# Stacked queries and doubled keys in a differential attention, with two background lanes paced anew

## The chip, the cores and the metric

The kernel runs on one core of one Trainium2 chip. The metric is the device time of one execution in microseconds (us). The core has five engines: TensorE for matrix products, VectorE, ScalarE, GpSimd and SyncE, the last of which only issues transfers here. In the profile they are PE (products) and PEld (weight loads), DVE, ACT, POOL and SP.

## What is computed

Two blocks in sequence on 512 tokens of width 1024, in float32. The first block has two layers: windowed attention, a short convolution and a state-space model (SSM) as three gated branches, then a gated feed-forward network. The second block, which the change mostly touches, has one layer: a gated linear unit into a causal depthwise convolution of 31 taps with a layer norm, beside it a causal differential attention, both gated and merged, then a feed-forward network.

```python
u = ua * jax.nn.sigmoid(ub)
u = conv31(u) + conv_b;  u = silu(layer_norm(u));  y_conv = u @ conv_w_out + conv_b_out
q1, q2, k1, k2 = rope(...)                      # 8 heads of 64 each
a = softmax(q1 k1^T) - lam * softmax(q2 k2^T)   # causal, per head
att = rms_norm(a @ v)                           # v: 8 heads of 128
y = (g_conv * y_conv + g_att * att) @ w_o
```

## The kernel before, in words

**Split products.** A float32 matrix is split into a rounded part h and a rest l, and a product is made of three: hh, hl and lh (`mm3`, line 467, products at lines 470 to 472). A split is one ScalarE rounding (line 380) and one VectorE subtraction (line 383). Weights come as units of 128x1024 through three buffers (`_fetch`, line 421); for most units of the second block's first half (`BESIDE`) the rest is made by two ScalarE operations and an accumulating transfer issued on GpSimd's queue, without VectorE.

**Buffers.** 78 slots of 128x512 float32 are handed out by `big` from a list of free ones, first freed first used. Eight PSUM banks are handed out by `psum`.

**The second block** (`second`, line 1372). The unit `w_in_2` gives the convolution's inputs (16 units). Then come four parts (line 1458), two heads of v each. In a part, 32 split products of 512 columns give the part's 4 query halves and 4 key halves (a block of 128 tokens by 8 x 64), `rope2` (line 1662) rotates them in place, 32 split products of 256 columns give v, and the part's attention is queued. After the fourth part stand 16 gates of 8 split products, then the eight output products of the convolution (conv_out), which read the normed convolution `cn`, then `w_o_2`.

**Lanes.** Convolution and attention run beside these products as Python generators, a step at a time. Every group of three products is a beat, every third beat a tick (`beat`, line 474; `tick`, line 496). At each tick a lane gains its rate as credit and does a step for each whole credit. `finish` runs all that is left of a lane at once. The lane conv (one generator at a time) holds eight `convolve` (line 1379; a step is three VectorE operations, ten steps each) and `conv_norm` (line 1771; 17 steps). The lane att (two at a time, by turns) holds for each part a `_diff_turn` (line 1680) and four `_diff_block` (line 1693). The rates are the constants of line 17: conv runs at R3 = 0.6 and R4 = 0.6, at R5 = 0.8 from the gates on; att at R2 = 1.0 and R6 = 1.5 from conv_out on. `finish("conv")` stands before conv_out (line 1499), `finish("att")` before conv_out's seventh output.

**Attention.** `_diff_turn` transposes the rotated 128x512 tiles, 16 transposes of 128x128 a part (line 1684), and splits the four results (two with queries, two with keys; a result holds two heads, one on the lower and one on the upper 64 rows). `_diff_block` n handles query block n against the n + 1 key blocks, w = 128 (n + 1) columns. For each of two s it makes three products a head on 64 rows (line 1712), alternating between two heads:

```python
for i, (x, y) in enumerate(((0, 0), (0, 1), (1, 0))):
    for e in range(2):
        rows = slice(64 * e, 64 * e + 64)
        nc.tensor.matmul(ps[e][:, :w], qk[s][x][rows, tn], qk[2 + s][y][rows, :w], start=i == 0, stop=i == 2)
```

Masks (line 552), exponentials, transposes of the probabilities (line 1736), products with v (line 1744), a norm and a last transpose (line 1762) follow.

**In the first block** the windowed attention stacks h and l of a query on 128 rows and multiplies them with keys that stand twice on 128 rows, two products a head (lines 993 and 994). The SSM (`ssm`, line 1152) spreads its input over partitions by 16 copies of 32x128, eight on ScalarE and eight on VectorE (line 1176), for each of four quarters ct.

**Order.** The program text is not the order of the engines' instructions. The kernel is built with a scheduler that orders every engine but SP's queue ahead of time, by text order among what its own timeline holds for ready. At run time each engine's order is fixed.

Of the kernel before, what the change touches and what calls it, by code (L numbers as in the profile page):

```python
# [16 lines left out]
R1, R2, R3, R4, R5, R6 = 0.9, 1.0, 0.6, 0.6, 0.8, 1.5  # L17
# [3 lines left out]
NTB = 4  # L21
# [290 lines left out]
class Net:  # L312
# [839 lines left out]
    def ssm(self, L, ct, u, tabs, ys2):  # L1152
# [18 lines left out]
        for i in range(4):  # L1171
            for j in range(4):
                o = uu[32 * j:32 * j + 32, i]
                s = u[32 * i:32 * i + 32, j::4]
                if j % 2:
                    nc.vector.tensor_copy(out=o, in_=s)  # L1176
                else:
                    self.act(o, s)
            if i == 1:
                yield  # L1180
# [191 lines left out]
    def second(self, follow, out):  # L1372
# [6 lines left out]
        def convolve(i):  # L1379
            acc = self.big(f"acc{i}")  # L1380
            self.act(acc, us[i], AF.Identity, scale=self.cw[:, 31 * i + 30:31 * i + 31], bias=self.p("conv_b", i))
            for j in range(29, -1, -1):
                s = 30 - j
                self.stt(acc[:, s:], us[i][:, :512 - s], self.cw[:, 31 * i + j:31 * i + j + 1], acc[:, s:], ALU.mult, ALU.add)
                if j % 3 == 0:
                    yield
            self.free(us[i])
            conv.append(acc)
            if i == 1:
                csum.append(self.big("csum"))  # L1390
                self.add(csum[0], conv[0], conv[1])
            elif i > 1:
                self.add(csum[0], csum[0], acc)

        csum, cn = [], []
        cl = self.lane("conv", 1, R3)
# [60 lines left out]
        self.lane("conv", 1, R4)  # L1457
        for part in range(4):
            pq = [self.psum(f"pq{t}") for t in range(NTB)]
# [11 lines left out]
            self.free(pq)  # L1471
            for t in range(NTB):
                self.rope2(ra[t], cos[:, t], sin[:, t])
# [18 lines left out]
            al.waiting += self.diff_attention(part, ra, vv, ya, done)  # L1492
            if part == 3:
                cl.waiting.append(self.conv_norm(conv, csum, cn))
                self.lane("conv", 1, R5)
# [4 lines left out]
        self.lane("att", 2, R6)  # L1500
# [161 lines left out]
    def rope2(self, a, cos, sin):  # L1662
# [9 lines left out]
        self.add(a, a, b)  # L1672
        self.free(b)

    def diff_attention(self, part, ra, vv, ya, done):
        qk = []
        left = [NTB]
        return [self._diff_turn(ra, qk)] + [self._diff_block(part, n, qk, vv, ya, left, done) for n in range(NTB)]

    def _diff_turn(self, ra, qk):  # L1680
        for j in range(4):
            pt = self.psum("qkT", (128, 4, 128))
            for t in range(NTB):
                self.nc.tensor.transpose(pt[:, t], ra[t].rearrange("p h d -> p (h d)")[:, 128 * j:128 * j + 128], self.ident)
            h, l = self.big("qkh", F32R), self.big("qkl", F32R)
            self.split(h, l, pt.rearrange("p t d -> p (t d)"))
            self.free(pt)
            qk.append((h, l))
            if j == 3:
                self.free(ra)  # L1690
            yield

    def _diff_block(self, part, n, qk, vv, ya, left, done):
        nc = self.nc
        while len(qk) < 4:
            yield
# [7 lines left out]

        pp = [[self.big("dp"), self.big("dp")] for _ in range(2)]
        mx = [self.small("dmx", (128, 2), bufs=4) for _ in range(2)]
        for s in range(2):
            ps = [self.psum("dsc") for _ in range(2)]
            for i, (x, y) in enumerate(((0, 0), (0, 1), (1, 0))):
                for e in range(2):  # L1710
                    rows = slice(64 * e, 64 * e + 64)
                    nc.tensor.matmul(ps[e][:, :w], qk[s][x][rows, tn], qk[2 + s][y][rows, :w], start=i == 0, stop=i == 2)  # L1712
# [17 lines left out]
        if n == NTB - 1:  # L1730
            self.free(qk)
# [39 lines left out]
    def conv_norm(self, conv, csum, out):  # L1771
        while len(conv) < 8:
            yield
        s = csum[0]
# [76 lines left out]
```

## Time and profile before

| | us |
|---|---|
| median of 3 runs | 2483.45 |
| lowest, highest | 2479.06, 2487.06 |
| profiled execution, its own time | 2489.97 |
| its span, first to last instruction | 2488.2 |
| PE busy in the span | 2442.6 |
| DVE busy | 1594.7 |
| ACT busy | 1111.5 |
| POOL busy | 362.5 |

Products overlap in the pipe: a product that the trace shows for 0.39 us starts 0.23 us after the one before. What a product takes is thus read from start to start. Mean granted clock of TensorE is 0.992 of full speed.

### The profile page before, as it was taken

How to read it: one execution, taken by the hardware profiler on the slowest of the kernel's cores; microseconds unless marked ns; L12 is line 12 of the kernel's file. 1: busy time of each engine (PE TensorE's matmuls, PEld its weight loads, DVE VectorE, ACT ScalarE, POOL GpSimd, SP SyncE). 2: the span in 40 equal slices, each digit the busy share in tenths (PEclk: the TensorE clock that was granted, in tenths of full speed). 3: DMA queues.
4: the chain of work that ended last, by engine and by line, in shares of the span. 5: the costliest groups of instructions: out<-in, count | busy, mean ns of one | idle time of the engine just before them, and what ended most of it. 6: DMA issues, size and time to landing. Idle time of an engine off the chain costs nothing.

```text
span 2488.2 us, 32578 instructions
## 1 busy us (share of the span) xinstructions
PE 2442.6 (98%) x12206; PEld 2054.3 (83%) x12206; DVE 1594.7 (64%) x3010; ACT 1111.5 (45%) x2034; POOL 362.5 (15%) x870
## 2 busy tenths in 40 slices
PE   8999999999999999999999999999999999999998
PEld 6888888888888888888888788988887769988887
DVE  7898855544455489875677744688788466643435
ACT  5467433322233365743432222544656765634222
POOL 7824000000037063200000000001111110000000
PEclk9999999999999999999999999999999989999999
DMA  4222233223233322123366632367646543122232
GB/s 154 80 77 69 77 123 106 93 94 102 93 99 109 120 70 79 60 102 121 130 208 223 216 120 94 116 168 182 147 102 140 119 106 119 69 93 89 93 106 77
DMA packets 90879, 282.80 MB, mean 114 GB/s; under 512 B 10336, under 2 KB 11744, under 8 KB 90720
## 3 DMA queue, kind: packets, MB, share of 16 engines
q1 hardware_dynamic: 83520, 254.50, 30.5%
q0 software_dynamic: 7200, 26.22, 6.2%
q8 instruction: 95, 1.56, 0.2%
q14 instruction: 64, 0.52, 0.1%
HBM read 274.39 MB, written 6.29 MB: 113 GB/s over the span
## 4 chain that ended last, share of the span: by engine, by line
PE 80%; DVE 7%; DMA 6%; issue 3%; ACT 2%; POOL 2%; SPq 1%; DVEq 0%; POOLq 0%; ACTq 0%
PE bank L470 25%; PE bank L471 25%; PE bank L472 25%; DMA slot<-in_wada_dram 4%; DVE slot L383 2%; DVE wl L383 2%; ACT slot L380 2%; PE bank L1712 1%; DVE slot L401 1%; DMA raw<-in_w_dram 1%; POOL s_w L383 1%; POOL slot L383 1%; PE bank L1744 1%; DVE slot L1176 0%; PE bank L1202 0%
## 5 line engine op out<-in xcount | busy, mean ns | idle before, releaser
L470 PE MATMUL bank<-slot,wh 128*128 128x512 f32 x2456 | 964.3, 394 | 7.8 <-ACT slot L380 7.6
L472 PE MATMUL bank<-slot,wl 128*128 128x512 f32 x2456 | 959.8, 391 | 4.2 <-DMA wl<-in_w_dram 2.1
L471 PE MATMUL bank<-slot,wh 128*128 128x512 f32 x2456 | 960.2, 391 | 0.0
L380 ACT ACTIVATE wh<-raw 128x1024 fp32r<-128x1024 f32 (+3 forms) x369 | 385.2, 1045 | 767.4 <-PE bank L471 390.6
L470 PEld LDWEIGHTS bank<-slot,wh 128*128 128x128 f32 x2456 | 463.4, 189 | 105.1 <-ACT slot L380 8.3
L472 PEld LDWEIGHTS bank<-slot,wl 128*128 128x128 f32 x2456 | 462.6, 188 | 104.5 <-DVE wl L383 4.9
L471 PEld LDWEIGHTS bank<-slot,wh 128*128 128x128 f32 x2456 | 463.4, 189 | 95.9 <-issue 1.7
L383 DVE TENSOR_TENSOR wl<-raw,wh 128x1024 fp32r<-128x1024 f32 (+3 forms) x319 | 390.9, 1226 | 203.0 <-ACT wh L380 201.6
L383 DVE TENSOR_TENSOR slot<-bank,slot 128x512 f32<-128x512 f32 (+4 forms) x340 | 197.6, 591 | 239.9 <-PE bank L472 208.7
L380 ACT ACTIVATE slot<-slot 128x512 fp32r<-128x512 f32 (+3 forms) x378 | 207.9, 558 | 288.9 <-DVE slot L383 265.9
L383 DVE TENSOR_TENSOR slot<-slot,slot 128x512 f32<-128x512 f32 (+4 forms) x480 | 287.0, 617 | 51.0 <-ACT slot L380 47.5
L380 ACT ACTIVATE slot<-bank 32x128 f32<-32x128 f32 (+8 forms) x398 | 183.2, 473 | 96.9 <-PE bank L472 34.5
L471 PE MATMUL bank<-wl,slot 128*128 128x512 f32 (+1 forms) x480 | 182.4, 380 | 4.3 <-DVE wl L383 4.3
L472 PE MATMUL bank<-wh,slot 128*128 128x512 f32 (+1 forms) x480 | 181.5, 379 | 0.0
L470 PE MATMUL bank<-wh,slot 128*128 128x512 f32 (+1 forms) x480 | 181.4, 380 | 0.0
L470 PE MATMUL bank<-slot,slot 128*128 128x256 f32 (+1 forms) x624 | 177.9, 293 | 2.1 <-ACT slot L380 2.1
L471 PE MATMUL bank<-slot,slot 128*128 128x256 f32 (+1 forms) x624 | 179.0, 291 | 0.5 <-DVE slot L401 0.5
L472 PE MATMUL bank<-slot,slot 128*128 128x256 f32 (+1 forms) x624 | 178.3, 289 | 0.0
L401 DVE SCALAR_TENSOR_TENSOR slot<-slot,slot 128x512 f32<-128x512 f32 (+1 forms) x184 | 123.9, 688 | 84.7 <-DMA slot<-in_wada_dram 57.2
L401 DVE SCALAR_TENSOR_TENSOR slot<-slot,cw,slot 128x485 f32<-128x485 f32 (+24 forms) x240 | 166.6, 732 | 4.2 <-ACT slot L380 2.4
L383 DVE TENSOR_TENSOR slot<-slot,bank 128x512 f32<-128x512 f32 (+1 forms) x104 | 66.1, 643 | 131.0 <-PE bank L472 131.0
L470 PEld LDWEIGHTS bank<-slot,slot 128*128 128x128 f32 x624 | 118.2, 193 | 4.4 <-ACT slot L380 2.7
(199 smaller groups left out, 2263.7 us busy)
## 6 DMA issues: line engine op xcount, KB each, us to landing
raw<-in_w_dram SPq DMA_DIRECT2D x373, 512.0 KB, 3.3
wl<-in_w_dram POOLq DMA_DIRECT2D x50, 512.0 KB, 5.6
slot<-in_wada_dram SPq DMA_DIRECT2D x96, 256.0 KB, 4.9
raw<-in_w_dram SPq DMA_DIRECT2D x32, 448.0 KB, 3.3
slot<-in_x_dram SPq DMA_DIRECT2D x16, 256.0 KB, 3.9
xd<-slot SPq DMA_DIRECT2D x16, 256.0 KB, 6.2
slot<-xd SPq DMA_DIRECT2D x16, 256.0 KB, 3.5
out_dram<-slot SPq DMA_DIRECT2D x8, 256.0 KB, 2.0
```

The costliest lines, as they stand in the source:

```text
L380: return self.nc.scalar.activation(out=out, in_=in_, func=func, scale=scale, **kw)
L383: return (eng or self.nc.vector).tensor_tensor(out=out, in0=a, in1=b, op=op)
L401: return self.nc.vector.scalar_tensor_tensor(out=out, in0=a, scalar=s, in1=b, op0=op0, op1=op1, **kw)
L470: t.matmul(ps, ah, bh, start=start, stop=False)
L471: t.matmul(ps, ah, bl, start=False, stop=False)
L472: t.matmul(ps, al, bh, start=False, stop=stop)
L1712: nc.tensor.matmul(ps[e][:, :w], qk[s][x][rows, tn], qk[2 + s][y][rows, :w], start=i == 0, stop=i == 2)
L1744: nc.tensor.matmul(po[:, e], at[e][:, b], vv[b // 2][:, b % 2, 128 * e:128 * e + 128], start=b == 0, stop=b == n)
```

## The change

Scores: the transposed queries are stored with h on one half of the rows and l on the other (`qs`), the keys are doubled on both halves before they are transposed (`kd`), and a head's score is two products on 128 rows. `_diff_turn` now makes 24 transposes a part and eight splits of 512 columns, four of them on 64 rows, in six steps (four before). `rope2` writes queries to half of a slot (two token blocks share one) and doubled keys to a slot each, and the projection's buffer is freed at once.

Pacing: att runs at R2 = 1.5 throughout. Conv runs in each part at the steps left over the ticks left up to 14 ticks into the gates, from the gates on at the steps left over 14, and at 0.7 once `conv_norm` begins.

First block: for ct = 0 all 16 copies of the SSM's input are on ScalarE.

```diff
-R1, R2, R3, R4, R5, R6 = 0.9, 1.0, 0.6, 0.6, 0.8, 1.5
+R1, R2, R3 = 0.9, 1.5, 0.6
...
-                if j % 2:
+                if j % 2 and ct:
                     nc.vector.tensor_copy(out=o, in_=s)
...
                 if j % 3 == 0:
+                    steps[0] -= 1
                     yield
...
+        steps = [80]
...
-        self.lane("conv", 1, R4)
         for part in range(4):
+
+            cl.rate = steps[0] / (16 * (4 - part) + 14)
...
+            qd, kd = [], []
             for t in range(NTB):
-                self.rope2(ra[t], cos[:, t], sin[:, t])
+                if t % 2 == 0:
+                    qd.append(self.big("qd", shape=(128, 2, 4, 64)))
+                kd.append(self.big("kd", shape=(128, 4, 2, 64)))
+                self.rope2(ra[t], qd[t // 2][:, t % 2], kd[t], cos[:, t], sin[:, t])
+                self.free(ra[t])
...
-                self.lane("conv", 1, R5)
+                cl.rate = steps[0] / 14
...
         self.finish("conv")
-        self.lane("att", 2, R6)
...
-        self.add(a, a, b)
+        self.add(q, a[:, 0:4], b[:, 0:4])
+        k, kb = (z[:, 4:8].unsqueeze(2).to_broadcast([128, 4, 2, 64]) for z in (a, b))
+        self.add(kd, k, kb)
...
+        for s in range(2):
+            pt = self.psum("qT", (128, 4, 128))
             for t in range(NTB):
-                self.nc.tensor.transpose(pt[:, t], ra[t].rearrange("p h d -> p (h d)")[:, 128 * j:128 * j + 128], self.ident)
...
+                self.nc.tensor.transpose(pt[:, t], qd[t // 2][:, t % 2, 2 * s:2 * s + 2].rearrange("p h d -> p (h d)"), self.ident)
+            src = pt.rearrange("p t d -> p (t d)")
+            qs = [self.big("qs", F32R) for _ in range(2)]
+            for e in range(2):
+                rows, rest = slice(64 * e, 64 * e + 64), slice(64 - 64 * e, 128 - 64 * e)
+                self.act(qs[e][rows], src[rows])
+                self.sub(qs[e][rest], src[rows], qs[e][rows].bitcast(F32))
             self.free(pt)
+            ks = []
+            for e in range(2):
+                yield
+                pt = self.psum("kT", (128, 4, 128))
+                for t in range(NTB):
+                    self.nc.tensor.transpose(pt[:, t], kd[t][:, 2 * s + e].rearrange("p i d -> p (i d)"), self.ident)
+                ks.append((self.big("kh", F32R), self.big("kl", F32R)))
+                self.split(*ks[e], pt.rearrange("p t d -> p (t d)"))
+                self.free(pt)
+            qk.append((qs, ks))
...
-            for i, (x, y) in enumerate(((0, 0), (0, 1), (1, 0))):
-                for e in range(2):
-                    rows = slice(64 * e, 64 * e + 64)
-                    nc.tensor.matmul(ps[e][:, :w], qk[s][x][rows, tn], qk[2 + s][y][rows, :w], start=i == 0, stop=i == 2)
+            for e in range(2):
+                for i in range(2):
+                    nc.tensor.matmul(ps[e][:, :w], qk[s][0][e][:, tn], qk[s][1][e][i][:, :w], start=i == 0, stop=i == 1)
...
     def conv_norm(self, conv, csum, out):
         while len(conv) < 8:
             yield
+        self.lanes["conv"].rate = 0.7
```

## Rows read from the trace of the kernel before

**Rows 1.** The page: busy us, share of the span, instructions.

```profile
PE 2442.6 (98%) x12206; PEld 2054.3 (83%) x12206; DVE 1594.7 (64%) x3010; ACT 1111.5 (45%) x2034; POOL 362.5 (15%) x870
```

**Rows 2.** Table by stretch: length, busy us (instructions), TensorE's granted clock, DMA.

```profile
1712.00:1976.00 264.00, 263.98 (x1456) 216.24 (x1455) 195.22 (x441) 155.30 (x333) 35.74 (x40) 1.00 0.56 129
1976.00:2000.00 24.00, 14.94 (x82) 11.61 (x81) 15.66 (x37) 20.31 (x45) 3.61 (x4) 0.79 0.32 74
2000.00:2066.00 66.00, 61.16 (x271) 45.64 (x270) 39.41 (x96) 39.65 (x92) 6.07 (x7) 0.96 0.48 132
```

**Rows 3.** TensorE's timeline, 1978 to 2066: start, length, instruction, [idle before, who ended it].

```profile
1992.08 0.69 PE L1712 MATMUL bank<-slot,slot 64*128 64x128 f32 x4 [4.50 <-DVE slot L383]
...
1995.62 0.80 PE L470 MATMUL bank<-slot,wh 128*128 128x512 f32 x1 [1.88 <-ACT slot L380]
...
2064.07 1.18 PE L1744 MATMUL bank<-slot,slot 128*128 128x128 f32 x6 [2.61 <-ACT slot L380]
```

**Rows 4.** TensorE's timeline, 1792 to 1797: six score products, then three.

```profile
1792.79 0.40 PE L472 MATMUL bank<-wh,slot 128*128 128x512 f32 x1
1793.12 0.96 PE L1712 MATMUL bank<-slot,slot 64*128 64x512 f32 x6
1794.01 0.50 PE L470 MATMUL bank<-wh,slot 128*128 128x512 f32 x1
...
1795.51 0.39 PE L470 MATMUL bank<-wh,slot 128*128 128x512 f32 x1
1795.83 0.96 PE L1712 MATMUL bank<-slot,slot 64*128 64x512 f32 x3
1796.72 0.50 PE L471 MATMUL bank<-wl,slot 128*128 128x512 f32 x1
```

**Rows 5.** Table by stretch, the products of line 1712 alone.

```profile
1712.00:2066.00 354.00, 37.32 (x192) 22.12 (x192) 0.98 0.53 125
```

**Rows 6.** TensorE's timeline, 129 to 132: stacked products of the first block's attention.

```profile
129.91 0.28 PE L993 MATMUL bank<-slot,slot 128*128 128x256 f32 x1
...
130.87 0.40 PE L470 MATMUL bank<-slot,wh 128*128 128x512 f32 x1
131.10 0.40 PE L471 MATMUL bank<-slot,wh 128*128 128x512 f32 x1
```

**Rows 7.** TensorE's timeline, 1746: four transposes of the turning and what follows.

```profile
1746.44 0.60 PE L1684 MATMUL bank<-cst,slot 128*128 128x128 f32 x4
1746.80 0.48 PE L470 MATMUL bank<-wh,slot 128*128 128x512 f32 x1
```

**Rows 8.** Groups by form, VectorE and ScalarE: busy us, mean ns | idle before.

```profile
L383 DVE TENSOR_TENSOR slot<-bank,slot 64x512 fp32r<-64x512 f32 x16 | 11.0, 688 | 1.2 <-ACT slot L380 0.8
L383 DVE TENSOR_TENSOR slot<-slot,slot 128x256 f32<-128x256 f32 x32 | 12.0, 417 | 1.1 <-ACT slot L380 1.1
L380 ACT ACTIVATE slot<-bank 64x512 fp32r<-64x512 f32 x16 | 9.5, 591 | 2.8 <-DVE slot L383 2.2 <-PE bank L963 0.4
```

**Rows 9.** Table by stretch, before and after the convolution's end.

```profile
1650.00:1920.00 270.00, 270.00 (x1461) 223.45 (x1459) 229.35 (x453) 146.64 (x281) 36.74 (x41) 1.00 0.62 146
1920.00:1980.00 60.00, 59.98 (x300) 47.51 (x300) 25.88 (x80) 41.12 (x94) 8.46 (x10) 1.00 0.62 134
```

**Rows 10.** VectorE's timeline: the copies for ct = 0 in layers 0 and 1.

```profile
42.37 8.29 DVE L1176 COPY slot<-slot 32x128 f32<-32x128 f32 x8
...
829.13 2.22 DVE L1176 COPY slot<-slot 32x128 f32<-32x128 f32 x8
```

**Rows 11.** Table by stretch around the copies of layer 0.

```profile
36.00:52.00 16.00, 12.44 (x56) 10.07 (x54) 11.99 (x13) 10.45 (x19) 16.00 (x56) 0.96 0.03 10
```

**Rows 12.** TensorE's timeline there.

```profile
52.70 0.79 PE L471 MATMUL bank<-wl,slot 128*128 128x512 f32 x1 [4.26 <-DVE wl L383]
```

**Rows 13.** ScalarE's timeline there.

```profile
39.87 4.23 ACT L380 ACTIVATE slot<-slot 128x512 f32<-128x512 f32 x9
```

**Rows 14.** All instructions that read the convolution's taps `cw`: min/median/max ns, first and last start.

```profile
L401 DVE SCALAR_TENSOR_TENSOR slot<-slot,cw,slot x240: 689/732/752, 1634.2 to 1919.2; 128x503 f32<-128x503 f32 x7, 128x497 f32<-128x497 f32 x7, 128x495 f32<-128x495 f32 x7, 128x493 f32<-128x493 f32 x7
```

More of the change, by code (lines that the diff above doesn't have):

```diff
@@ L1491, in second @@
                 ya[m] = self.big(f"ya{m}")
-            al.waiting += self.diff_attention(part, ra, vv, ya, done)
+            al.waiting += self.diff_attention(part, qd, kd, vv, ya, done)
             if part == 3:
                 cl.waiting.append(self.conv_norm(conv, csum, cn))
-                self.lane("conv", 1, R5)
+                cl.rate = steps[0] / 14
             for m in range(sum(GATES[:part]), sum(GATES[:part + 1])):
@@ L1671, in rope2, with diff_attention, _diff_turn @@
         self.mul(a, a, tab(cos))
-        self.add(a, a, b)
+        self.add(q, a[:, 0:4], b[:, 0:4])
+        k, kb = (z[:, 4:8].unsqueeze(2).to_broadcast([128, 4, 2, 64]) for z in (a, b))
+        self.add(kd, k, kb)
         self.free(b)
-    def diff_attention(self, part, ra, vv, ya, done):
+    def diff_attention(self, part, qd, kd, vv, ya, done):
         qk = []
         left = [NTB]
[L1678 to L1682, printed above, removed]
+        return [self._diff_turn(qd, kd, qk)] + [self._diff_block(part, n, qk, vv, ya, left, done) for n in range(NTB)]
+    def _diff_turn(self, qd, kd, qk):
+        for s in range(2):
+            pt = self.psum("qT", (128, 4, 128))
             for t in range(NTB):
-                self.nc.tensor.transpose(pt[:, t], ra[t].rearrange("p h d -> p (h d)")[:, 128 * j:128 * j + 128], self.ident)
-            h, l = self.big("qkh", F32R), self.big("qkl", F32R)
-            self.split(h, l, pt.rearrange("p t d -> p (t d)"))
-            self.free(pt)
-            qk.append((h, l))
-            if j == 3:
-                self.free(ra)
+                self.nc.tensor.transpose(pt[:, t], qd[t // 2][:, t % 2, 2 * s:2 * s + 2].rearrange("p h d -> p (h d)"), self.ident)
[5 more added lines that the diff above has]
+                self.sub(qs[e][rest], src[rows], qs[e][rows].bitcast(F32))
+            self.free(pt)
+            ks = []
[8 more added lines that the diff above has]
+            qk.append((qs, ks))
+            if s == 1:
+                self.free(qd, kd)
             yield
@@ L1694, in _diff_block @@
         nc = self.nc
-        while len(qk) < 4:
+        while len(qk) < 2:
             yield
@@ L1730, in _diff_block @@
         if n == NTB - 1:
-            self.free(qk)
+            self.free([[q, k] for q, k in qk])
         at = []
```

2 lines of the change are left out of this document (1 added, 1 removed).

## The prediction

> **What bounds the kernel now.** I read the page's busy shares first: TensorE is busy for 98% of the span [rows 1], so a microsecond counts only if it comes off TensorE's own row of products or off one of its few waits. The change sits almost wholly in one stage, so next comes the table by stretch from the first query-key product of the second block (1712) to the last product of conv_out (2066) [rows 2]. Up to 1976 TensorE is never idle (263.98 of 264). From 1976 to 2000 it works 14.94 of 24 us at a mean granted clock of 0.79, from 2000 to 2066 61.16 of 66 at 0.96. That is 9.1 + 4.8 = 13.9 us idle. The clock costs at most 24 x 0.21 + 66 x 0.04 = 7.7 us more, part of it inside the idle time; I count 4. So about 18 us are lost at the end of the stage. The TensorE timeline names the waits [rows 3]: 4.50 us for VectorE in the middle of a score product, 1.88 us for ScalarE before conv_out's first product at 1995.62, 2.61 us for ScalarE among the last attention blocks. The reader is to see two regimes: a long stretch in which only TensorE's work counts, and a short end in which waits count too.
>
> **Where the end comes from.** The step counts of the lanes follow from the code. A convolution is 8 x 10 steps and its norm 17; an attention part has 4 steps of turning and 6 for each of 4 blocks, and a few idle steps. A tick is three beats: 16 ticks a part, 43 in the 16 gates. At rates 0.6 and 0.8 the gates begin with 54 convolution steps issued and end with 80, plus 9 of the norm; attention (1.0) stands at 48 and then 91 of 121. So finish("conv") empties 8 norm steps in one go, and conv_out, whose input they are, waits; 28 attention steps lie under conv_out and the last ones are emptied at once before m = 6. That is the timeline's picture: the norm chain and part 3's first blocks contend at 1980 to 1996, the last blocks at 2061.
>
> **Part 1, the score products.** Today each pair of heads takes six products on 64 rows. Six at 512 columns started together hold the array from 1792.79 (start of the product before) to 1794.01 (start of the one after), less one normal interval of 0.23: 0.99 us. Three alone, one head's share, hold it from 1795.51 to 1796.72: 0.98 us [rows 4]. So pairing is free when it happens, and often it doesn't: the engines' order is set ahead of time and splits many pairs. The whole x192 hold 37.32 us [rows 5]. After the change there are 128 products over all 128 rows, of the form that the first block's attention uses already (lines 993 and 994): eight of 256 columns run from 129.91 to 130.87, 0.12 each, and a 512-column product takes 0.23 (130.87 to 131.10) [rows 6]. With 0.12 for 128 columns too (a bound from above) and 0.17 for 384 (halfway), four products cost 0.48, 0.48, 0.68 and 0.92 for n = 0 to 3, 2.56 together, times 8 (two s, four parts) = 20.5 us. Gain 37.3 - 20.5 = **16.8 us**, all on the path. Bounds: were every pair undivided today, the groups would cost 0.99 / 0.92 x 20.5 = 22 us by the 512-column one, so the gain is at least 1.5 us; at the top, 0.11 instead of 0.12 for the narrow ones gives 17.5.
>
> One rule of the Trainium skill speaks against this part. TensorE: Matmul & The Clock Gate, Part 3 (Packing small matmuls), says that products on different row groups run at the same time, starting some 4 ns apart. By it six half-height products cost three intervals, 3 x (0.12 + 0.12 + 0.17 + 0.23) x 8 = 15.4 us, and the change would lose 5 us instead of gaining 17. The trace agrees with the concurrency but not with the price: 0.99 us against 3 x 0.23 [rows 4], because the first product starts 0.33 after its predecessor, not 0.23 (1792.79 to 1793.12), and three alone are no cheaper than six. By the skill's other page on it, TensorEngine Tiling (Array Packing), Key Properties, a change of tiling mode drains the engine; that would be such a delay.
>
> **Part 2, the transposes.** Doubled keys make 24 transposes a part of 16: 32 more. Four of them take 0.36 us (1746.44 to 1746.80) [rows 7], 0.09 each, and with 0.12 as the upper end **+3.4 us** at 0.105.
>
> **Part 3, more VectorE and ScalarE work.** Turning grows from four splits to eight a part, so 16 more subtractions at 688 ns (11 us) and 16 more activations at 591 ns (9.5 us); writing the queries apart adds 16 additions of 128x256 at 417 ns (6.7 us) [rows 8]; the doubled-key addition replaces the old 512-column one. TensorE covers this as long as VectorE keeps pace. VectorE works 229.35 of 270 us (85%) from 1650 to 1920 while TensorE is idle for nothing, and then only 25.88 of 60 [rows 9]: the convolution is through, and attention is issued too slowly to use it. Slots are used more heavily too (twelve of split operands for eight, six of rotated ones for four, though a rotated buffer is freed at once). No row shows a slot wait by itself; bounds are 0 and one 4.50-us wait [rows 3] a part, 18 us. I take 0, since TensorE had no idle time while two parts were in flight.
>
> **Part 4, the pacing.** With attention at 1.5 and the convolution at what is left over what remains (0.82 in part 0, 0.83 later, 0.79 in the gates), the gates begin with 69 convolution steps and 74 attention steps and end with 80, all 17 of the norm (three ticks before) and all 137 of attention. So nothing is emptied in one go at finish("conv"), and conv_out runs without attention beside it: the 2.61-us wait goes, and most of the 1980 to 1996 burst. What is late next is the tail of the norm: its last step is issued three ticks (some 8 us) ahead of conv_out and is a chain of six operations of the size of those in [rows 8]. Of the 18 us I take **12** away (bounds 0 and 18). The new price is VectorE's. Its need from 1650 to conv_out's first product is now 229.4 + 25.9 + some 10 = 265 us; 18 come with the new work, and 18 with the attention moved ahead of conv_out (about half of the 39.41 us in 2000 to 2066 [rows 2]): 301 us. The stretch is 1995.6 - 1650 = 346 us today, plus 17 for the attention moved in (66 less 4.8 idle less 192 products at 0.23), less 16.8, plus 3.4, less the 9.1 of waits: about 341. VectorE must hold 88% where it held 85% unhurried. For that I add **+2 us** (bounds 0 and +15).
>
> **Part 5, the copies of the first block.** For ct = 0 eight VectorE copies a layer go to ScalarE. In layer 0 the eight take 8.29 us, in layer 1 2.22 us [rows 10]; GpSimd works without a gap during the first, 16.00 of 16 us [rows 11]. The split of a weight stands behind them on VectorE, and TensorE waits 4.26 us for it [rows 12]. ScalarE's nine operations, eight of them copies, took 4.23 us there [rows 13], so eight more take 3.8, and the weight's rounding behind them slips by up to that: the wait moves to ScalarE but shrinks. I take **-4 us**, bounds -7 (the whole wait, with the clock at half for what follows) and +1.
>
> **The sum.** -16.8 + 3.4 - 12 + 2 - 4 = -27.4 us. On the profiled execution (2489.97 us, of which the span is 2488.2) that gives 2462.6; it lies 6.5 above the median of the runs shown, so on the median 2483.45 - 27.4 = **2456 us**.
>
> **Rivals.** (a) The end stays as it is. The engines' order is set ahead from readiness, not from the lanes alone: the last of the convolution's products began at 1919.2 [rows 14], some 30 us before the lanes had issued the last of them. If pacing moves little, or VectorE holds only its 85% (301 / 0.85 = 354 us, 13 later), the gain is 16.8 - 3.4 + 4, less 0 to 4: 2466 to 2470. For it: 88% is above anything in the table. Against: both lanes end earlier by count. Chance 0.24. (b) The change doesn't do what it says: half-height pairs would have run at three intervals (the rule above), scores and transposes cost 8.5 us, pacing gives 12 and copies 4, less 2: 2478, no measurable change. Against it stand the 37.32 us. Chance 0.03; with other ways to within 0.3%, 0.07. (c) Slower: VectorE becomes the bound. The convolution, issued a third faster, fills VectorE's queue; masks, splits and the norm line up behind it, and TensorE's queue, which runs in order, stands at scores or at conv_out. From 1712 to 2066 VectorE's mean share is 250.3 / 354 = 71% [rows 2]; at that share 301 us need 424, 83 more than the stretch has, and the result is 2456 + 81 = 2537. It decides below 301 / (341 + 35) = 80%, where 2491 is reached. For it: order on an engine is fixed, and one late result holds all behind it. Against: from 1650 to 1920 the same mix held 85% with no wait. Chance 0.06. Upside (d): the whole end and the whole copy wait vanish: 2445, chance 0.13 for 2441 to 2448.
>
> **How the numbers follow.** Forecast 0.50 (2448 to 2464), (d) 0.13, (a) 0.24, same 0.07, slower 0.06. The range 2441 to 2472 holds the forecast, (d) and most of (a). A measurement of this kernel tells about 0.3% (7.5 us) from no change, so faster means below 2476: 0.87, same 0.07, slower 0.06.
>
> **What would show it.** In the profile after: no products of 64 rows, x128 full-height ones with about 20 us; 96 transposes at the turning line; VectorE's low share from 1920 to 1980 gone; TensorE busy and at full clock up to conv_out, no attention after it; at 48 to 53 us a shorter wait, now for ScalarE. I am wrong if VectorE shows over 90% before conv_out and TensorE waits for it, or if the waits at conv_out's first product are as long as before.

## The result and the profile after

The changed kernel takes 2503.76 us (median of 4 runs, 2501.22 to 2504.58) against 2483.74 us for the kernel before: a ratio of 1.0078 [1.0061, 1.0094]. It is about 20 us **slower**; forecast were 2456 us and a gain of 27. The profiled execution has a span of 2502.0 us, 13.8 more than before.

The page of the changed kernel, busy time by engine (before in [rows 1]):

```profile
PE 2437.4 (97%) x12174; PEld 2061.6 (82%) x12174; DVE 1598.9 (64%) x3026; ACT 1129.7 (45%) x2066; POOL 363.0 (15%) x870
```

TensorE is busy 5 us less, and the span is 14 us longer: waits were added. Where they lie is in the table by stretch (length, busy us of each engine, granted clock, DMA share, GB/s), first from the parts to the first gates, then to the end of conv_out's stage:

```profile
1715.00:1885.00 170.00, 150.19 (x866) 129.88 (x865) 146.96 (x334) 97.13 (x215) 18.81 (x20) 0.93 0.46 112
1885.00:1970.00 85.00, 83.38 (x463) 70.56 (x463) 59.25 (x143) 57.13 (x132) 13.31 (x15) 1.00 0.47 106
1970.00:2085.00 115.00, 104.08 (x484) 84.42 (x482) 63.30 (x141) 79.71 (x162) 14.39 (x17) 0.94 0.61 156
```

In the first stretch, where TensorE never idled before [rows 2], it now idles 19.8 us, and its mean clock is 0.93; at the end stand another 10.9 us. The end was about as bad before (13.9 us from 1976 to 2066), so the loss is new idle time **in the parts**, at a place that the prediction took for free.

What the score products were to save is there. TensorE's timeline of the changed kernel, two products of 256 and two of 128 columns with a neighbour on each side:

```profile
1751.53 0.39 PE L470 MATMUL bank<-wh,slot 128*128 128x512 f32 x1
1751.75 0.33 PE L1735 MATMUL bank<-slot,slot 128*128 128x128 f32 x2
1751.92 0.45 PE L471 MATMUL bank<-wl,slot 128*128 128x512 f32 x1
...
1757.75 0.39 PE L471 MATMUL bank<-wl,slot 128*128 128x512 f32 x1
1757.98 0.40 PE L1735 MATMUL bank<-slot,slot 128*128 128x256 f32 x2
1758.21 0.40 PE L472 MATMUL bank<-wh,slot 128*128 128x512 f32 x1
```

From the neighbour's start to the next neighbour's, less one interval of 0.23: 0.16 us for the pair of 128, 0.23 for that of 256. With 0.36 and 0.45 for 384 and 512 (found in the same way at 1921 and 1941), a head costs 1.20 us, times 16 (two heads, two s, four parts) 19.2 us: the 20.5 of the sum, and no more half-height products. Counted as busy time, like the 37.32 us of [rows 5], the row after shows 31.44 us for its 128 products, because busy time counts what overlaps in the pipe. Counted from start to start, 122 of the 192 products before, those in groups between dense foreground products, hold 23.3 us, which makes some 37 for all of them (an estimate). So 37 and 19.2 are like for like.

Where TensorE idles in the parts is in its timeline of 1861 to 1880:

```profile
1861.41 0.39 PE L472 MATMUL bank<-wh,slot 128*128 128x512 f32 x1
1861.64 0.51 PE L1735 MATMUL bank<-slot,slot 128*128 128x384 f32 x2
1861.99 0.60 PE L1767 MATMUL bank<-slot,slot 128*128 128x128 f32 x4
1862.43 0.27 PE L1785 MATMUL bank<-cst,slot 128*128 128x128 f32 x1
1862.81 0.73 PE L1735 MATMUL bank<-slot,slot 128*128 128x512 f32 x2
1863.37 0.27 PE L1785 MATMUL bank<-cst,slot 128*128 128x128 f32 x1
1863.40 0.59 PE L1735 MATMUL bank<-slot,slot 128*128 128x384 f32 x2
1865.98 0.82 PE L1735 MATMUL bank<-slot,slot 128*128 128x512 f32 x2 [1.99 <-DVE dmx L552]
1867.10 0.73 PE L1785 MATMUL bank<-cst,slot 128*128 128x128 f32 x2 [0.30 <-ACT slot L380]
1867.48 2.63 PE L1735 MATMUL bank<-slot,slot 128*128 128x384 f32 x6
1875.74 1.54 PE L1759 MATMUL bank<-cst,slot 128*128 128x128 f32 x6 [5.64 <-DVE slot L401]
1877.22 1.65 PE L1767 MATMUL bank<-slot,slot 128*128 128x128 f32 x6
1878.66 1.06 PE L1708 MATMUL bank<-cst,slot 128*128 128x128 f32 x4
1879.38 0.56 PE L470 MATMUL bank<-slot,slot 128*128 128x256 f32 x1
```

Between the last query-key product (1861.41) and the first v product (1879.38) TensorE's order holds 18 us of attention and nothing else: scores, then a wait for masks, then 5.64 us until VectorE has merged the exponentials for the transposes of line 1759. The v products stand behind. They read nothing of the attention, but they aren't free of it, because buffers go to whom asks next in the order in which they came free. The list of PSUM banks, written out while the program is put together, gives the first v product the bank that the second head's transposes of line 1759 (from 1875.74) fill. And three of the part's four query-key results are copied out into slots that the attention has just given back. ScalarE's timeline has such a copy:

```profile
1878.38 0.60 ACT L380 ACTIVATE slot<-bank 128x512 f32<-128x512 f32 x1 [0.34 <-DVE slot L401]
```

It reads a bank alone, which TensorE had filled by 1861; what it waits for at VectorE is therefore its slot. A second long wait is at 1801.67, where TensorE stands 5.48 us for a weight's rest, which comes by a transfer.

### The profile page after: what moved, and what is told of

Read it like the earlier page. It is cut to its first block, busy times and chain, and to the rows that moved or that the text cites. A ratio compares the mean times of both kernels' runs of the same rounds, so it can differ in the third digit from the quotient of the medians.

```text
span 2502.0 us, 32568 instructions
## 1 busy us (share of the span) xinstructions
PE 2437.4 (97%) x12174; PEld 2061.6 (82%) x12174; DVE 1598.9 (64%) x3026; ACT 1129.7 (45%) x2066; POOL 363.0 (15%) x870
## 5 line engine op out<-in xcount | busy, mean ns | idle before, releaser
L383 DVE TENSOR_TENSOR slot<-bank,slot 128x512 f32<-128x512 f32 (+4 forms) x356 | 208.7, 597 | 239.8 <-PE bank L472 208.7
L380 ACT ACTIVATE slot<-slot 128x512 fp32r<-128x512 f32 (+4 forms) x394 | 215.2, 553 | 301.8 <-DVE slot L383 276.1
L383 DVE TENSOR_TENSOR slot<-slot,slot 128x512 f32<-128x512 f32 (+4 forms) x496 | 292.8, 611 | 56.7 <-ACT slot L380 52.8
L380 ACT ACTIVATE slot<-bank 128x512 f32<-128x512 f32 (+7 forms) x414 | 191.5, 478 | 110.4 <-PE bank L472 33.6
L401 DVE SCALAR_TENSOR_TENSOR slot<-slot,cw,slot 128x507 f32<-128x507 f32 (+28 forms) x240 | 165.1, 731 | 1.7 <-ACT slot L380 0.9
```

Of the source, the lines that this page charges most:

```text
L380: return self.nc.scalar.activation(out=out, in_=in_, func=func, scale=scale, **kw)
L383: return (eng or self.nc.vector).tensor_tensor(out=out, in0=a, in1=b, op=op)
L401: return self.nc.vector.scalar_tensor_tensor(out=out, in0=a, scalar=s, in1=b, op0=op0, op1=op1, **kw)
```

## The experiments

Ratios are to the kernel before, timed beside each run; "us" in the text is a difference of ratios times 2484, unless medians are named. Idle is TensorE's from 1715 to 1885 us, the 170 us less its busy time. Rates are the attention's in parts / gates / output.

| kernel | scores | convolution | attention | median us | ratio, 95% interval | idle us |
|---|---|---|---|---|---|---|
| before | old | old | 1.0/1.0/1.5 | 2483.74 | 1 | 0.0 |
| conv_only | old | new | 1.0/1.0/1.5 | 2480.75 | 0.9983 [0.9974, 0.9992] | 0.4 |
| p10_g15 | old | new | 1.0/1.5/1.5 | 2481.80 | 0.9976 [0.9962, 0.9990] | 0.6 |
| late_conv | old | new, one buffer | 1.0/1.0/1.5 | 2496.44 | 1.0047 [1.0015, 1.0078] | 5.6 |
| att15_only | old | old | 1.5/1.5/1.5 | 2514.21 | 1.0126 [1.0105, 1.0147] | 12.7 |
| p15_g10 | old | new | 1.5/1.0/1.5 | 2511.87 | 1.0099 [1.0067, 1.0131] | 16.9 |
| pacing_only | old | new | 1.5/1.5/1.5 | 2509.12 | 1.0098 [1.0083, 1.0113] | 18.0 |
| pre_pacing | old | new, early buffers | 1.5/1.5/1.5 | 2510.97 | 1.0118 [1.0086, 1.0150] | 17.6 |
| p15_g8 | old | new | 1.5/0.8/1.5 | 2497.42 | 1.0056 [1.0038, 1.0074] | 18.5 |
| changed | new | new | 1.5/1.5/1.5 | 2503.76 | 1.0078 [1.0061, 1.0094] | 19.8 |
| new_att_old_conv | new | old | 1.5/1.5/1.5 | 2526.58 | 1.0166 [1.0151, 1.0181] | 18.9 |
| f_p15_g8 | new | new | 1.5/0.8/1.5 | 2483.08 | 0.9978 [0.9962, 0.9994] | 18.5 |
| f_p14_g10 | new | new | 1.4/1.0/1.5 | 2499.15 | 1.0035 [1.0015, 1.0054] | 9.3 |
| pre_after | new | new, early buffers | 1.5/1.5/1.5 | 2513.65 | 1.0118 [1.0087, 1.0148] | 18.5 |
| pre_f8 | new | new, early buffers | 1.5/0.8/1.5 | 2495.87 | 1.0045 [1.0021, 1.0069] | 20.9 |
| raw4_after | new | new | 1.5/1.5/1.5 | 2505.12 | 1.0084 [1.0069, 1.0099] | 17.7 |
| raw4_f8 | new | new | 1.5/0.8/1.5 | 2498.07 | 1.0055 [1.0040, 1.0070] | 18.2 |
| half_taps | new | half the taps | 1.5/1.5/1.5 | 2485.23 | 0.9999 [0.9989, 1.0009] | 16.0 |
| w1_p10_g12 | new | new | 1.0/1.2/1.5, one at a time | 2535.34 | 1.0210 [1.0194, 1.0225] | 18.6 |
| copies_only | old | old | 1.0/1.0/1.5 | 2490.06 | 1.0024 [1.0014, 1.0035] | 1.6 |

**Which part of the change is it?** Three theories: V (VectorE is overfull through the faster convolution), A (attention at 1.5 puts waiting products ahead in TensorE's order) and S (the new form's buffers and splits).

att15_only is the kernel before with its first line, conv_only with the lines under it; pacing_only has both; new_att_old_conv is the changed kernel with the convolution's old rates.

```diff
 # att15_only
-R1, R2, R3, R4, R5, R6 = 0.9, 1.0, 0.6, 0.6, 0.8, 1.5
+R1, R2, R3, R4, R5, R6 = 0.9, 1.5, 0.6, 0.6, 0.8, 1.5
 # conv_only
...
+            cl.rate = steps[0] / (16 * (4 - part) + 14)
...
-                self.lane("conv", 1, R5)
+                cl.rate = steps[0] / 14
...
+        self.lanes["conv"].rate = 0.7
```

> The kernel before with the new rates of both lanes alone (no stacked scores, no moved copies). Theories: V, VectorE's queue is overfull because the convolution is issued faster; A, attention at 1.5 puts products that wait for other engines ahead of the projection in TensorE's order; S, the stacked form's extra slots and splits make the waits. V and A: the waits in the parts (about 28 us more than before from 1712 to 1880) are here too, and without the 15 us that the stacked products save net, so 2500 to 2520 us. S: no such waits, and the end shorter, 2465 to 2480 us.

> The kernel before with the convolution's new rates alone; attention at 1.0 and 1.5 as before. V: 2490 to 2510, with TensorE waiting in the parts for weights or for VectorE. A and S: 2475 to 2488, as before or a little better at conv_out's first product.

> The kernel before with the attention lane alone at 1.5 from the first part on; convolution rates as before. V: within 8 us of before (2476 to 2490), little idle TensorE from 1712 to 1880. A: 2495 to 2515, TensorE idle 10 to 20 us in that stretch. S: 2470 to 2484.

> The changed kernel with the convolution's rates put back to 0.6, 0.6 and 0.8. V: the waits in the parts go, 2460 to 2475 us, faster than before. A and S: they stay, 2495 to 2510.

The table by stretch of conv_only:

```profile
1715.00:1885.00 170.00, 169.59 (x982) 141.46 (x981) 147.66 (x317) 94.46 (x202) 19.26 (x21) 1.00 0.47 113
```

VectorE is busy for 147.66 of 170 us (87%) here, as in the changed kernel (146.96), and TensorE idles 0.4 us: V falls for this stretch. The pacing alone, without the new form, costs 24 us: S isn't needed. The attention's rate alone costs 31 us. A holds; the convolution's new rates are a gain of 4 alone. new_att_old_conv came out above both of its ranges.

**In the parts, or at the end?** A1 says that the loss arises within the parts; A2 that it arises at conv_out, where no attention is left beside the convolution's norm. p15_g10 and p10_g15 are conv_only with a rate of 1.5 in the parts alone, or in the gates alone; the other two are the changed kernel with less attention in the gates.

```diff
 # p15_g10: R2 = 1.5; p10_g15: R2 = 1.0 and 1.5 here
                 cl.rate = steps[0] / 14
+                al.rate = 1.0
 # f_p15_g8; f_p14_g10 has R2 = 1.4 and 1.0 here
                 cl.rate = steps[0] / 14
+                al.rate = 0.8
...
         self.finish("conv")
+        al.rate = 1.5
```

> The old form of the scores and the new rates of the convolution, as in conv_only, with the attention at 1.5 steps in the four parts alone: at 1.0 as before while the gates run, 1.5 in the convolution's output. conv_only stands at 2480.8 us, pacing_only (1.5 from the parts to the end) at 2509.1. Theory A1 (the 28 us arise within the parts: the attention's products are put ahead of the parts' own in TensorE's order before their operands are ready): about 2505. Theory A2 (they arise at the end: no attention is left beside the convolution's norm and output, so their chains stand bare): some attention is left for the gates and the output, so about 2485 to 2490, with few more waits from 1712 to 1880 than conv_only.

> The mirror of p15_g10: the attention at 1.0 in the parts as before, 1.5 in the gates and the output, with the new rates of the convolution. A1: 2479 to 2484, as conv_only. A2: the attention is used up or nearly so when the output's first product stands waiting for the norm; 2495 to 2505. If both runs cost about half of the 28 us, both places count.

> The changed kernel whole, with the attention at 1.4 in the parts, 1.0 in the gates and 1.5 in the output instead of 1.5 throughout. It has the new form, so its clean score products are worth about 18 us. A1: the parts' waits stay, so 2498 to 2503. A2: the end gets its cover back; 2478 to 2485.

> The changed kernel whole, with the attention at 1.5 in the parts, 0.8 in the gates and 1.5 in the output: as much attention as it can be given after the gates without touching the parts. A1: 2500 to 2505, the same as the changed kernel. A2: 2478 to 2488, and less idle TensorE after 1970 us than the changed kernel's.

The same stretch of p15_g10, and then of p10_g15:

```profile
1715.00:1885.00 170.00, 153.08 (x861) 126.55 (x859) 138.77 (x316) 93.31 (x216) 17.69 (x20) 0.93 0.41 103
```

```profile
1715.00:1885.00 170.00, 169.38 (x987) 141.17 (x987) 147.44 (x317) 95.85 (x205) 20.14 (x22) 1.00 0.49 120
```

In the old form A1 holds: 1.5 in the parts costs 29 us over conv_only, and 1.5 in the gates nothing. Of the kernels with the old form, those at 1.0 idle 0 to 1.6 us in the parts (5.6 in late_conv, below), those at 1.5 12.7 to 18.5. How the thin order avoids it shows in conv_only's timeline of TensorE, first at the same place (the last query-key product and the first v product of the last part), then at the same time of the span, when its gates have begun. The rows left out after 1864.97 are gate products (lines 470 to 472):

```profile
1839.32 0.39 PE L472 MATMUL bank<-wh,slot 128*128 128x512 f32 x1
1839.64 0.77 PE L1714 MATMUL bank<-slot,slot 64*128 64x128 f32 x7
1840.34 0.38 PE L470 MATMUL bank<-slot,slot 128*128 128x256 f32 x1
...
1863.37 0.94 PE L1746 MATMUL bank<-slot,slot 128*128 128x128 f32 x6
1864.24 0.80 PE L1714 MATMUL bank<-slot,slot 64*128 64x384 f32 x6
1864.97 0.50 PE L470 MATMUL bank<-slot,wh 128*128 128x512 f32 x1
...
1870.18 0.73 PE L1714 MATMUL bank<-slot,slot 64*128 64x512 f32 x2
```

Here 1 us of attention stands between the query-key and the v products, not 18. Later come short groups of attention, with 5 us of gate products between them in which the masks and exponentials are made. No wait is shown.

A2 counts too where the gates run at 0.8: f_p15_g8 is 25 us below the changed kernel (21 by the medians), with nearly the same idle time in the parts. Its table by stretch at the end:

```profile
1970.00:2085.00 115.00, 111.48 (x650) 97.04 (x649) 70.80 (x158) 87.74 (x192) 12.99 (x16) 1.00 0.59 151
```

Idle falls from 10.9 to 3.5 us, and the clock rises from 0.94 to 1.00. The three other pairs of 0.8 against 1.5 in the gates have the same sign: p15_g8 against pacing_only -10, raw4_f8 against raw4_after -7, pre_f8 against pre_after -18. The two pairs of 1.0 against 1.5 show nothing: p15_g10 is level with pacing_only, conv_only 2 us above p10_g15. f_p14_g10 lies in A1's range, but not as A1 has it: its idle time in the parts is down to 9.3 us, and another 20 stand in 1885 to 1970, most of them in one wait (below). What can stand bare without that attention is read in att15_only's timeline of TensorE, where conv_out starts:

```profile
2027.31 2.07 PE L627 MATMUL bank<-slot,ones 128*128 128x512 f32 x2 [3.62 <-DVE slot L397]
2040.15 1.65 PE L470 MATMUL bank<-slot,wh 128*128 128x512 f32 x3 [10.76 <-ACT slot L380]
```

The norm's chain (a variance, a spread, eight scalings and splits) takes 14.4 us of TensorE's time with nothing beside it. But att15_only also has the convolution's old rates, by which steps of the norm are left for finish("conv"). In the changed kernel no such wait is left: from 1885 to 2085 line 627 waits 1.2 us and no product of line 470 more than 0.23. Its longest wait there is one of the attention's own products:

```profile
2014.90 1.22 PE L1767 MATMUL bank<-slot,slot 128*128 128x128 f32 x4 [4.36 <-ACT djk L380]
```

So the bare norm is shown for att15_only alone; why the changed kernel loses at its end stays open.

**Why does TensorE idle in the parts?** Three causes were tried: a late start of the fifth convolution, VectorE's load, and late weights.

*A buffer's history (theory L).* Buffers are handed out first freed first used. The list of free buffers, written out while the program is put together, shows that in pacing_only the fifth convolution's sum gets one that part 0's attention has just given back, in conv_only one that a weight gave back long before. ScalarE's timeline has its first operation at 1757.73 and at 1727.03. pre_pacing and pre_after take this buffer a convolution ahead; late_conv gives conv_only a buffer of the attention.

```diff
 # pre_pacing, pre_after
-            acc = self.big(f"acc{i}")
+            acc = early.pop() if early else self.big(f"acc{i}")
+            if 3 <= i < 7:
+                early.append(self.big(f"acc{i + 1}"))
 # late_conv, ahead of the first line
+            if i == 4:
+                self.free_slots.insert(0, self.free_slots.pop(8))
```

> pacing_only (2509.1 us) with one thing changed: the fourth to seventh convolution take the buffer for the next one's sum along when they start, a convolution ahead, so it's one that was given back long ago. Theory L (buffer lineage): with the attention at 1.5 the fifth convolution's sum gets a buffer that part 0's attention block has just given back, so it can't start before that block has run; its first operation on ScalarE stands at 1757.7 in pacing_only and at 1727.0 in conv_only, VectorE has no taps in between, and they are crowded into 1760 to 1880 later. By L the first operation comes at about 1727 and the time falls by 15 to 28, to 2481 to 2494. Theory A1 without L (the attention's density alone): no change, 2505 to 2512.

> The changed kernel (2503.8) with the buffers of the sums taken one convolution ahead. L: the fifth convolution begins some 30 us earlier (1761.1 in the changed kernel), the idle time of TensorE from 1765 to 1880 (20 us) falls to a few, and the time to 2480 to 2490. A1 without L: 2500 to 2506.

> The other way round: conv_only (2480.8), the attention at its old rates, with the fifth convolution's sum put into a buffer that an attention block gave back six ticks before instead of one of a weight given back fifteen before. L: its first operation moves from 1727 to about 1755 to 1765, VectorE's taps crowd behind it, and the time rises by 8 to 25, to 2489 to 2506. A1 without L: no change, 2478 to 2484.

ScalarE's timeline of pre_pacing, then of late_conv, the fifth convolution's first operation:

```profile
1669.51 0.80 ACT L380 ACTIVATE slot<-slot,slot,cw 128x512 f32<-128x512 f32 x1
```

```profile
1760.23 0.80 ACT L380 ACTIVATE slot<-slot,slot,cw 128x512 f32<-128x512 f32 x1
```

In pre_pacing it starts 88 us earlier, and nothing is won: 17.6 us of idle time, 2511 us. pre_after and pre_f8 came out 10 and 17 us above the kernels that they were made from, outside both ranges. So this buffer does not explain the loss at 1.5. In late_conv it starts 33 us later than in conv_only (24 counted from the first convolution's start, which is later too), and that edit alone costs 16 us where attention is thin. One buffer's history is thus worth as much as most effects here, and a single pair of kernels that differ by less than some 15 us proves little; only what repeats over pairs does. Nor is it one buffer alone. TensorE's wait of 15.11 us in f_p14_g10, at 1901.63, is for ScalarE, whose timeline has:

```profile
1901.09 0.98 ACT L380 ACTIVATE slot<-bank 128x384 f32<-128x384 f32 x2 [13.93 <-DVE slot L383]
```

This copy reads a bank alone, too, and waits 13.93 us for VectorE, so for its slot; by the list of buffers the rotation's subtractions (line 383) give it back. Here a slot wait in the new form is shown.

*VectorE's load (V2) or the attention's own chain (D)?* half_taps leaves out every second tap.

```diff
-                self.stt(acc[:, s:], us[i][:, :512 - s], ..., acc[:, s:], ALU.mult, ALU.add)
+                if j % 2:
+                    self.stt(acc[:, s:], us[i][:, :512 - s], ..., acc[:, s:], ALU.mult, ALU.add)
```

> The changed kernel with every second tap of the second block's convolution left out (120 of 240 VectorE operations, some 77 us of that engine at a start-to-start interval of 0.64 us; steps and pacing are unchanged). It separates two readings of the idle TensorE between 1715 and 1885 us (20 us in the changed kernel). Theory V2 (VectorE is crowded there: taps stand ahead of masks and splits): with half of the taps gone the idle time falls below 6 us and the whole time to 2475 to 2485. Theory D (density: the attention's own chain, product to mask to exponential to transpose, is too long for the pace at which its products are put ahead in TensorE's order, whatever else VectorE does): 12 to 20 us stay, and the time is 2492 to 2503.

half_taps' table by stretch, and its timeline of TensorE at the place shown above:

```profile
1715.00:1885.00 170.00, 154.04 (x897) 133.75 (x898) 117.42 (x288) 97.27 (x221) 19.12 (x22) 0.94 0.44 108
```

```profile
1861.60 1.22 PE L1736 MATMUL bank<-slot,slot 128*128 128x512 f32 x2 [0.69 <-DVE dmx L552]
1862.62 0.71 PE L1786 MATMUL bank<-cst,slot 128*128 128x128 f32 x2
1862.98 3.15 PE L1736 MATMUL bank<-slot,slot 128*128 128x384 f32 x6
1869.77 1.54 PE L1760 MATMUL bank<-cst,slot 128*128 128x128 f32 x6 [3.63 <-DVE slot L401]
```

VectorE's share falls to 69%, and 16 of 20 us stay idle, at the same place and for the same operations. So V2 isn't what makes most of the idle time in the parts, and what remains is an order in which the attention's chain stands alone, from scores to mask to exponential to merge to transpose, three engines long. Why the order is so isn't settled. D says that too many of its steps are issued.

A rival that no run tests is the hand-out of buffers, which half_taps leaves as it was. The lists of five kernels at 1.5 were written out (att15_only, p15_g10, pacing_only, the changed kernel and half_taps): the first v products of the last part stand directly behind 33 to 43 products and transposes of the attention, and their bank was the attention's. In before, conv_only and p10_g15 they stand behind 0 to 7, and theirs was one that the query-key products gave back. Density and hand-out go together in these; a kernel at 1.5 with a bank set apart for v would part them.

D's range for the time (2492 to 2503) was missed: the whole time does fall by 20 us, but most of it after 1885, where the convolution is through earlier (from 1970 to 2085 half_taps idles 6.1 us at a clock of 0.99, the changed kernel 10.9 at 0.94): by the time alone V2 would have been believed, and only the stretch tells them apart. VectorE's load does cost time, then, but mainly after the parts.

*Late weights (W).* In the changed kernel the transfers' queue waits 18.8 us at one place for VectorE to subtract a weight of v out of a raw buffer, and TensorE 5.48 us later on. raw4_after has a fourth raw buffer.

```diff
-    SLOTS = 78
+    SLOTS = 76
-            self.rings[name] = [[self.cp.tile([128, 1024], dt, name=f"{name}_{i}") for i in range(3)], 0]
+            self.rings[name] = [[self.cp.tile([128, 1024], dt, name=f"{name}_{i}") for i in range(4 if name == "raw" else 3)], 0]
```

> The changed kernel with four raw buffers for the weights' transfers instead of three (and 76 slots, since a raw buffer takes the place of two). Theory W: the transfers' queue, which waits 18.8 us at one place for VectorE to subtract a weight of v out of a raw buffer, no longer does, the waits of TensorE for the weights' rests (7.3 + 2.9 us, the longest 5.5) fall below 3, and the time to 2493 to 2498. If the weights were only late beside something else that is late too (V2 or D), the waits change their name: 2500 to 2505.

The waits for weights' rests on line 471 fall from 7.3 to 2.4 us, but the idle time only from 19.8 to 17.7, and the time not at all (1.0084 against 1.0078): a symptom. raw4_f8 came out 19 us above f_p15_g8 and above both of its ranges, so the buffer is no gain there either.

**What is the form worth, and can it run thin?** p15_g8 is the old form at f_p15_g8's pacing. w1_p10_g12 is the changed kernel with a thin attention.

```diff
 # w1_p10_g12; its gates run at 1.2, the output at 1.5
-        al = self.lane("att", 2, R2)
+        al = self.lane("att", 1, 1.0)
```

> The old form of the scores at exactly the pacing of f_p15_g8 (convolution at what is left, attention 1.5 in the parts, 0.8 in the gates, 1.5 in the output). It gives the price of the form at an equal pacing: if the score products' 18 us and the transposes' 3.7 come through, it stands 10 to 15 above f_p15_g8, at 2493 to 2498; if the form's gain is eaten by its own work on VectorE and ScalarE, within 5 of it, 2480 to 2488. It also tells the end from the parts in the old form: with the parts' 28 us still there it is about 2505.

> The changed kernel with the attention one generator at a time instead of two, at 1.0 in the parts, 1.2 in the gates and 1.5 in the output: as thin in the parts as before (30 steps a part at 1.0; the pair at 1.5 takes 36 in 24 ticks), which the 78 slots allow in this order. Theory D (density): TensorE's idle time from 1715 to 1885 falls from 20 to below 6 us, and with the form worth 14 (f_p15_g8 against p15_g8) the time is 2462 to 2472, below both kernels. If the form's own VectorE and ScalarE work brings the idle time at any pace: 12 to 20 us stay, 2478 to 2490.

At this pacing the form is worth 19 us (14 by the medians), as the sum of scores and transposes had it (13.4). But in the other pairs at equal pacing it is worth 5 (changed against pacing_only), 0 (pre_after against pre_pacing) and -10 (new_att_old_conv against att15_only): so cheaper products on TensorE are not always time. w1_p10_g12 came out 63 us above the range expected. A reading that its trace fits, but no run tests, is that with one generator at a time each chain stands alone, without a second to fill its waits. Its timeline of TensorE:

```profile
1804.39 1.54 PE L1761 MATMUL bank<-cst,slot 128*128 128x128 f32 x6 [6.41 <-DVE slot L401]
```

So it isn't density in steps a tick alone: at 1.0 in the parts TensorE idles 18.6 us. The new form with two generators at 1.0 was not tried: the 78 slots don't hold it (1.4 is the least that they do, and there the idle time is 9.3 us, with the slot wait of 15.1 us at 1901). That the form would pay in full under a thin attention stays open.

**The copies.**

```diff
-                if j % 2:
+                if j % 2 and ct:
```

> The kernel before with the eight copies for ct = 0 moved to ScalarE and nothing else. The prediction put this at -4 us (-7 to +1), 2479.5. The changed kernel's trace has a wait of 2.00 us for ScalarE and one of 1.19 us for VectorE in the place of the 4.26 us, and stands level with the kernel before at 215 us: by that 2482 to 2485, within the scatter of the kernel before.

Below, with the last step.

## Why the prediction was wrong, step by step

**Part 1 and Part 2, scores and transposes: right on TensorE's row.** 19.2 us for 20.5 forecast, and four transposes take 0.36 us after as before. The sum took a busy time (37.32) less a time from start to start (20.5); that the two agree for the products before (some 37 either way) was luck, since after the change they are 31.44 and 19.2. By the Trainium skill's TensorE: Matmul & The Clock Gate, Part 3 (products on different row groups run at the same time), the form would have been 5 us dearer; the trace does not agree: from start to start the products hold some 37 us before and 19.2 after. What failed is the clause "all on the path". That was so where TensorE never idled; with the new pacing it idles there.

**Part 4, the pacing: the step that failed.** Forecast -12 + 2, measured +24 without the new form. VectorE's need was right (301 us forecast, 304.18 measured from 1650 to conv_out's first product at 2034), but the stretch was 384 us, not 341. First, the argument took [rows 2] (264 us without idle time) as slack to be filled, and priced the denser attention in VectorE's share alone. The idle-free stretch went with the old rate: v and gate products stood between an attention block's steps and hid its chain. At 1.5 the chain stands bare, 13 to 20 us, whether VectorE is at 86% or 69%. Second, "conv_out runs without attention beside it" was counted as a gain. Its size was wrong: from 1970 to 2085 TensorE idles 10.9 us in the changed kernel and 13.9 in the kernel before, at a clock of 0.94 and 0.93. And the four kernels that keep attention back by a rate of 0.8 in the gates are 7 to 25 us faster than those at 1.5. From a count of steps the wrong thing was read: when a step is issued is not when its operands, or its buffers, are ready. Neither sign of being wrong came: VectorE is at 86% in the parts, and conv_out's first product waits at most 0.23 us (1.88 before). The signs looked at the end, and the loss was in the parts.

**Part 3, "no slot wait; I take 0".** Its reason (no idle time before) was no reason for the new form: f_p14_g10 has a slot wait of 13.93 us on ScalarE, 15.11 on TensorE, and one buffer's history cost 16 us in late_conv. What slots and banks cost the changed kernel itself isn't known. The v weights, whose subtractions are VectorE's, held the transfers' queue up by 18.8 us, but by raw4_after that was a symptom.

**Part 5, the copies: mis-sized.** Forecast -4 (-7 to +1), measured +6 in copies_only (0.14 to 0.35%). The mechanism went as described; TensorE's timeline of copies_only, for 4.26 us of [rows 12]:

```profile
49.31 1.39 PE L470 MATMUL bank<-wh,slot 128*128 128x512 f32 x5 [2.17 <-ACT wh L380]
...
51.80 0.79 PE L471 MATMUL bank<-wl,slot 128*128 128x512 f32 x1 [1.10 <-DVE wl L383]
```

The wait moves to ScalarE and the rest of it stays with VectorE, 3.27 us together: 1 us won, not 4. VectorE's subtraction, no longer late for the copies, is late for the rounding. Where the whole time then loses is not settled; the profiled execution is 3.1 us longer than that of before.

**Rival (c)** had the sign, at a chance of 0.06, but not the mechanism: VectorE was to be the bound, below a share of 80%. conv_only holds 87% with 0.4 us of idle time, and VectorE's mean share from 1650 to conv_out is 79% in the changed kernel, just under the 80% at which (c) was to decide; but by half_taps the waits in the parts don't come from VectorE's load. Rival (a) came nearest in spirit (the order is set ahead, so the lanes' counts move little), but it saw no loss in that.

## What to carry to other kernels

A stretch without idle time is a balance, not slack: before a background lane is made denser, look at which foreground products stand between its steps, and whether its chain across the engines fits into them. Ask, too, whose buffers the foreground will be handed, since a product that reads nothing of the background can still wait for its bank. Background work kept for the place where the foreground has a chain of its own, such as a norm ahead of its first reader, gained 7 to 25 us in four pairs here, and nothing in the two with a smaller difference of rates. Where a scheduler lays out the order anew with every edit, believe an effect that repeats over pairs, and read its stretch, before a single difference of times.

## What the runs showed of the hardware

Idle time cost TensorE twice. The changed kernel's timeline, after a wait of 1.94 us that ends at 1851.18:

```profile
1854.63 0.80 PE L471 MATMUL bank<-wl,slot 128*128 128x512 f32 x1 [1.83 <-DMA wl<-in_w_dram]
1855.22 0.63 PE L472 MATMUL bank<-wh,slot 128*128 128x512 f32 x1
1855.65 0.63 PE L470 MATMUL bank<-wh,slot 128*128 128x512 f32 x1
...
1859.81 0.40 PE L470 MATMUL bank<-wh,slot 128*128 128x512 f32 x1
1860.04 0.39 PE L471 MATMUL bank<-wl,slot 128*128 128x512 f32 x1
```

The query-key products that follow the two waits start 0.43 us apart until 1859.5 and 0.23 after that. The granted clock is 0.50 from 1855.0 to 1859.4 and 0.98 from 1859.6 to 1861.0, the lower and the higher of the two clocks (1.2 and 2.4 GHz); the mean granted clock from 1715 to 1885 is 0.93, and 1.00 in each kernel that idles under 2 us there. That is why TensorE's busy time from 1712 to the stage's end at 2085 (the three rows above and 3.00 before them, 340.65 us) is no less than the 340.08 of [rows 2], though the products had become some 14 us cheaper (about 2 of the 340.65 us are the next stage's first products): most of what the form saved, the clock took.
